# vs and u by seven products each: where late adding transfers, statistics, small constants and weight sums stand in their queues

## The chip, the cores and the metric

The kernel runs on one core of one Trainium2 chip, in one launch. The metric is the device time in microseconds. Times before are the median of 3 runs; the profile is one further execution, with its own time.

## The reference

One layer of a streaming-encoder block on a sequence of 1024 tokens with 1024 features, in float32:

```python
h = rmsnorm(x, norm_g)
q, k, v, za, u, vs, zs, gm = split(h @ w_in)
a = (window_sink_attention(rope(q), rope(k), v, sinks) * silu(za)) @ w_att_out
vs = layernorm(gelu(vs), sg_ln_g, sg_ln_b)                 # along its 1024 features
mixed = einsum('gij,bnjgc->bnigc', masked(sg_w), vs) + sg_b  # 8 groups, blocks of 128 tokens
sgo = (gelu(u) * mixed * silu(zs)) @ w_sg_out
ga, gs = sigmoid(gm + b_merge)
out = rmsnorm(x + (ga * a + gs * sgo) @ w_o, final_g)
```

The mask makes the quarter of each 128 x 128 matrix of `sg_w` zero in which the first 64 tokens would see the last 64.

## The kernel before

Every large product is done by a scheme of Strassen's kind: both factors are cut into 2 x 2 quarters, and seven products of quarters, of sums and of differences of them take the place of eight. The products are called by the form of h that they use: `b11`, `t1`, `t2`, `b21`, `t3`, `b22`, `t4`. Each factor is split into a high part (a cast, ScalarE, line 155) and the rest (a subtraction, VectorE, line 156), and each product takes high x high, high x low and low x high. `product` (line 341) is one such product of 12 matmuls of 128 x 512.

The stages that the change touches, in order:

*vs* (lines 463 to 857). h is formed tile by tile. Its token tiles 4 to 7 give `raw_sum` and `raw_b21`; `add_on` is a transfer on GpSimd's queue that adds to what lies at its target. `raw_t2(t)` (line 603) adds to `raw_sum` on VectorE, and then adds this to `raw_b21` by such a transfer. The quarter `s3` of vs's weights is loaded and gets another quarter added in the same way, in two transfers. `keep_t5` (line 700) copies a product from PSUM into the place of `raw_sum`, so it waits until raw_t2's transfer has read that place. Then come three rounds of `late_product` (matmuls on line 668), with `t2`, `t3` and `t4`: in each, two halves of the weights go over four tiles of tokens. `to_x12` (line 805) and `to_x22` (line 808) add the accumulator to what is kept or subtract it; the next round writes into the same accumulators and waits for them. `aside` is a list of steps on the other engines, one after each group of matmuls: splits of the weights, forms of h for the next round (lines 567 and 568), gelu with the statistics for layernorm (`bn_stats`, line 778). The mixing matrices `mix_w` are loaded early, their masked quarter is set to zero by a memset (line 789), and they are split for the sums of their rows (line 844).

*u* (lines 858 to 939). Eight row tiles of weights in four pairs, `gemm_pair` for each: seven products, in this order, `acc` being one PSUM bank that four of them share:

```python
product(acc, b11); x11 = copy(acc)         # ScalarE, line 359
product(t5, t1);   x22 = -t5               # ScalarE, line 363
product(acc, t2);  x12 = copy(acc)         # ScalarE, line 366; before t3 may write acc
product(t2, b21);  x11 += t2               # VectorE, line 371, term[0]
product(acc, t3);  x22 -= acc              # VectorE, line 376; before t4 may write acc
product(t5, b22);  x12 += t5               # VectorE, line 380
product(acc, t4);  x21 = -acc
```

`finish` applies gelu (line 921) and puts a mix on the list `late`. Between the products, `hook` takes two steps from `late`: first the second statistics of eight tiles and their means (line 866), then `normalize` (a square root on ScalarE, line 135, and eight passes over vs on VectorE, line 871), then mixes: four small matmuls into a bank of two (line 893), gain and bias (line 901), the product with u (line 909) and a store on SP's queue. `split_next` splits the next weights; before it takes the second unit of a pair it makes the four sums of that pair's quarters, s1 to s4 (`sums`, lines 242 to 245), on VectorE. The weights come through three tiles, so a tile of the pair after next is loaded when the splits and sums that read its predecessor are done. `pace` holds a transfer back until a given step.

After u the sinks of the attention are loaded in two transfers (line 932), multiplied by -1 into `nsink` (line 937), and `b_merge` is loaded (line 938); all are used in later stages. Then follow k and v, q, the attention and the rest.

What runs when: a scheduler orders the instructions of each engine from the program's order and its own estimates; `after(second, first)` fixes that the second stands behind the first in their engine's queue, without a wait. Each engine, SP's and GpSimd's transfer queues too, works its queue off in order. TensorE multiplies, VectorE is shown as DVE, ScalarE as ACT, GpSimd as POOL, SyncE as SP.

Of the kernel before, what the change touches and what calls it, by code (L numbers as in the profile page):

```python
# [27 lines left out]
ALU = mybir.AluOpType  # L28
# [24 lines left out]
def hybrid_tile(  # L53
# [16 lines left out]
    nc = tc.nc  # L70
# [8 lines left out]
    def nm(s):  # L79
        count[0] += 1  # L80
        return f"{s}_{count[0]}"

    def bank(tag, dt=F32):
        return psum.tile([P, 512], dt, name=nm("ps_" + tag), tag="ps_" + tag, bufs=2)

    def mtile(shape, dt, tag, bufs, pool=None):
        return (pool or main).tile(shape, dt, name=nm(tag), tag=tag, bufs=bufs)
# [7 lines left out]
    def xtile():  # L95
        return mtile([P, HALF], F32, "x", 5)
# [13 lines left out]
    sink_sb = const.tile([P, 8], F32, name="sink_sb")  # L110
    nsink_sb = const.tile([P, 8], F32, name="nsink_sb")
    bm_sb = const.tile([P, 16], F32, name="bm_sb")
    lg_sb = const.tile([P, KC], F32, name="lg_sb")
    lb_sb = const.tile([P, KC], F32, name="lb_sb")
# [33 lines left out]
    def split(hi, lo, src, minus=False):  # L148
        if minus:
            nc.scalar.mul(hi, src, -1.0)  # L150
            nc.vector.scalar_tensor_tensor(
                lo, src, -1.0, hi.bitcast(F32), op0=ALU.mult, op1=ALU.subtract
            )
        else:
            nc.scalar.copy(hi, src)  # L155
            return nc.vector.tensor_sub(lo, src, hi.bitcast(F32))  # L156

    def after(second, first):

        tc.add_manual_dep(  # L160
            second.ins,
            first.ins.name,
            mybir.DependencyInfo(mybir.DependencyClass.NoSync, mybir.DependencyReason.DATA),
            reason="order",
        )
# [36 lines left out]
    def begin_job():  # L202
        n = len(begun)
        if n < written[0]:
            begun.append(n)
            units.extend(jobs[n]())

    def split_next():

        if not units:  # L210
            begin_job()
        if not units:
            return
        halves, keys = units.pop(0)
        if keys[0][1] == 2:
            make_sums()
        hi = mtile([P, D], F32R, "wh", 3)
        lo = mtile([P, D], F32R, "wl", 3)
        if isinstance(halves, list):
            for c, half in enumerate(halves):  # L220
                split(hi[:, half_of(c)], lo[:, half_of(c)], half)
        else:
            wide = halves.shape[1]
            first = split(hi[:, 0:wide], lo[:, 0:wide], halves)
            if keys[0] == (done[0] - 1, 6) and done[0] > LAST_OF_Q + 2:
                make_sums(first)
        for c, key in enumerate(keys):
            ready[key] = hi[:, half_of(c)], lo[:, half_of(c)]
        if len(units) == 1:
            begin_job()  # L230

    def half_of(half):
        return slice(half * HALF, (half + 1) * HALF)
# [19 lines left out]
    def make_sums(first=None):  # L253

        while sums_to_make:
            sums_to_make.pop(0)(first)
# [23 lines left out]
    def paced(move):  # L280

        if pace[0] is not None:
            tc.add_manual_dep(
                move.ins,
                pace[0].ins.name,
                mybir.DependencyInfo(mybir.DependencyClass.Sync, mybir.DependencyReason.DATA),
                reason="pace",
            )
# [39 lines left out]

    done = [0]
    term = [None]  # L330
    LAST_OF_Q = 8

    def product(acc, part, form, fresh, last=True):
# [16 lines left out]
    def gemm_pair(b, finish, hook=lambda: None, second="o"):  # L350

        n = done[0]
        done[0] += 1
        acc = bank("mm")[:]
        x11, x12, x22 = xtile(), xtile(), xtile()
        product(acc, ready[n, 0], b["b11"], True)
        pace[0] = nc.scalar.copy(x11[:], acc)
        hook()  # L360
        t5 = bank("o")[:]
        product(t5, ready[n, 2], b["t1"], True)
        pace[0] = nc.scalar.mul(x22[:], t5, -1.0)
        hook()
        product(acc, ready[n, 3], b["t2"], False)
        pace[0] = nc.scalar.copy(x12[:], acc)  # L366
        split_next()
        hook()
        t2 = bank(second)[:]
        product(t2, ready[n, 1], b["b21"], True)  # L370
        term[0] = nc.vector.tensor_add(x11[:], x11[:], t2)
        finish(0, 0, x11, x11[:], 1.0)
        split_next()
        hook()
        product(acc, ready[n, 4], b["t3"], False)
        term[0] = nc.vector.tensor_sub(x22[:], x22[:], acc)  # L376
        finish(1, 1, x22, x22[:], 1.0)
        hook()
        product(t5, ready[n, 5], b["b22"], False)
        term[0] = nc.vector.tensor_add(x12[:], x12[:], t5)  # L380
        finish(0, 1, x12, x12[:], 1.0)
        split_next()
        hook()
        product(acc, ready[n, 6], b["t4"], False)
        finish(1, 0, xtile(), acc, -1.0)
        split_next()
        hook()
# [93 lines left out]
    xh = mtile([P, NT, D], F32, "xh", 1, gelu)  # L481
    stats = mtile([P, NT, 2, 6], F32, "bn", 1, gelu)
# [32 lines left out]
    def x_place(i, j, t):  # L515
        return xh[:, 4 * j + t % 4, half_of(i)]
# [4 lines left out]
    def raw_sum(t):  # L521
        return x_place(0, 1, t)

    def raw_b21(t):
        return x_place(1, 0, t)

    g_of = list(g_in)
    casts, lows, turns = [], [], []

    def add_on(dst, src):  # L530
        nc.gpsimd.dma_start(dst, src, accum_op=ALU.add)

    def behind(move, first):
        tc.add_manual_dep(
# [66 lines left out]

    def raw_t2(t):
        nc.vector.tensor_add(raw_sum(t), raw_sum(t), f22[0][:, t - 4, :])
        add_on(raw_b21(t), raw_sum(t))

    def w_vs(i, j, c):
        return w[W_VS + 4 * i + 2 * j + c]

    def two_k(v, c):
        return v[:, 2 * c : 2 * c + 2, :]  # L610

    def flat(v):
        return v.rearrange("p k n -> p (k n)")

    raws = {}
# [13 lines left out]
    def pair_of_w():  # L629
        return mtile([P, D], F32R, "wh", 3), mtile([P, D], F32R, "wl", 3)  # L630

    def keep_w(name, c, hi, lo):
        for k in range(2):
            vs_w[name, 2 * c + k] = hi[:, half_of(k)], lo[:, half_of(k)]

    def split_w(name, c, src=None, behind=False):
        hi, lo = pair_of_w()
        (split_behind if behind else split)(hi[:], lo[:], flat(two_k(raws[name], c)) if src is None else src)
        keep_w(name, c, hi, lo)
# [111 lines left out]
    for t in range(4):  # L751
        to_x11(t)
    for t in (5, 6, 7):
        raw_t2(t)
    load_part("s3", "t4h", 1, 0, True)
    for c in range(2):
        add_on(flat(two_k(raws["s3"], c)), w_vs(0, 0, c))
    by_s4(0)
    by_s4(1)
    a22 = []  # L760
# [14 lines left out]
        keep_t5(t)  # L775

    def statistics(t, half):
        nc.vector.bn_stats(stats[:, t, half, :], xh[:, t, half_of(half)])

    def gelu_of(t, half=0):  # L780
        two = xh[:, t : t + 2, half_of(half)]
        after(nc.scalar.activation(two, two, AF.Gelu), last_cast)
        if half == 0:
            for i in range(2):
                statistics(t + i, 0)

    mix_w = mtile([P, KC, P], F32, "wT", 1, pool)
    behind(nc.sync.dma_start(mix_w[:], sg_w), turns[-1])
    nc.vector.memset(mix_w[64:128, :, 0:64], 0.0)
    ones = mtile([P, P], F32R, "ones", 1, pool)  # L790
    nc.vector.tensor_scalar(ones[:], ident[:], 0.0, 1.0, op0=ALU.mult, op1=ALU.add)

# [35 lines left out]
        + [lambda: gelu_of(0), lambda: gelu_of(2)],  # L828
    )
    row_sums = [bank("sc") for half in range(2)]  # L830
    split_w("s3", 1)
    wh, wl = pair_of_w()
    split(wh[:], wl[:], mix_w[:].rearrange("p g i -> p (g i)"))
    late_product(
# [9 lines left out]
            nc.tensor.matmul(row_sums[half][:], ones[:], part[:, half_of(half)], start=n == 0, stop=n == 1)  # L844
    split_w("a22", 1, a22[1][:])
    part_of_early(1)
    paced(nc.sync.dma_start(lg_sb[:], ln_g))
    paced(nc.sync.dma_start(lb_sb[:], ln_b))
    begin_job()
    late_product("t4", "a22", to_x21, [split_next, lambda: gelu_of(4, 1), lambda: gelu_of(6, 1)])  # L850
    for _ in range(2):
# [7 lines left out]
    def hook():  # L859
        for _ in range(2):  # L860
            if late:
                late.pop(0)()
# [55 lines left out]
    for m in range(0, KC, 2):  # L918

        def finish(i, half, q, src, sign, m=m):  # L920
            nc.scalar.activation(q[:], src, AF.Gelu, scale=sign)
            late.append(lambda: mix(m + i, half, q))
# [3 lines left out]
        gemm_pair(hb, finish, both)  # L926
    while late:
        late.pop(0)()
    of_head = sinks.rearrange("(c e r) -> e c r", e=2, r=2)
    for e in range(2):  # L930
        paced(
            nc.sync.dma_start(
                sink_sb[e * 64 : (e + 1) * 64].rearrange("p (c r) -> p c r", r=2),
                of_head[e].partition_broadcast(64),
            )
        )
    nc.vector.tensor_scalar_mul(nsink_sb[:], sink_sb[:], -1.0)
    paced(nc.sync.dma_start(bm_sb[:], b_merge))
    stage.close()


# [751 lines left out]
    for p in range(4):  # L1693
        acc = bank("sc" if p < 2 else "mm")[:]
        x11 = mtile([P, HALF], F32, gtag(), 1, pool)
# [14 lines left out]
    for p in range(4):  # L1710
        n, t, acc, x11 = N_PAIRS + p, T_ORDER[p], accs[p], firsts[p]
# [173 lines left out]
```

## Time and profile before

| | |
|---|---|
| time, median of 3 runs | 935.46 us (934.58 to 936.62) |
| profiled execution, own time | 937.09 us |
| its span, first to last instruction | 935.3 us |
| mean granted TensorE clock | 0.988 |
| TensorE busy | 903.3 us, 97% of the span |
| VectorE, ScalarE, GpSimd busy | 697.5, 526.4, 141.1 us |
| moved by DMA | 209.57 MB, mean 224 GB/s |

In the views, a row of a timeline gives start and length in us, engine, line, operation, what is written and read, and in brackets how long the engine had stood idle just before, with what ended that. A row of waits gives the engine and line that waited, what ended the wait, the sum in us, how many times, and the longest. A row of windows gives a stretch, its length, the busy time of each engine with its instructions, the granted TensorE clock, the share of time that the DMA engines were busy, and GB/s.

### The profile page before, as it was taken

How to read it: one execution, taken by the hardware profiler on the slowest of the kernel's cores; microseconds unless marked ns; L12 is line 12 of the kernel's file. 1: busy time of each engine (PE TensorE's matmuls, PEld its weight loads, DVE VectorE, ACT ScalarE, POOL GpSimd, SP SyncE). 2: the span in 40 equal slices, each digit the busy share in tenths (PEclk: the TensorE clock that was granted, in tenths of full speed). 3: DMA queues.
4: the chain of work that ended last, by engine and by line, in shares of the span. 5: the costliest groups of instructions: out<-in, count | busy, mean ns of one | idle time of the engine just before them, and what ended most of it. 6: DMA issues, size and time to landing. Idle time of an engine off the chain costs nothing.

```text
span 935.3 us, 13186 instructions
## 1 busy us (share of the span) xinstructions
PE 903.3 (97%) x4284; PEld 749.5 (80%) x4284; DVE 697.5 (75%) x1263; ACT 526.4 (56%) x1058; POOL 141.1 (15%) x204
## 2 busy tenths in 40 slices
PE   8998899979999999999999999999998999999996
PEld 6786778858888778888888888888886887888885
DVE  6868676545668667788878888746798489669996
ACT  6856423323444356776766676746565565458443
POOL 2222112212111001111111111101100011210012
PEclk9999989989999999999999999999999999999999
DMA  9987677974878776778797778899868764999633
GB/s 297 231 216 191 214 225 165 173 149 138 279 236 265 240 210 156 204 201 195 196 221 225 248 216 202 225 290 385 290 237 310 257 200 153 297 290 309 203 109 116
DMA packets 131598, 209.57 MB, mean 224 GB/s; under 512 B 12649, under 2 KB 61033, under 8 KB 131530
## 3 DMA queue, kind: packets, MB, share of 16 engines
q1 hardware_dynamic: 110072, 149.74, 48.5%
q0 software_dynamic: 21312, 58.73, 28.0%
q8 instruction: 34, 0.56, 0.2%
q14 instruction: 34, 0.28, 0.1%
q10 hardware_dynamic: 146, 0.27, 0.1%
HBM read 147.74 MB, written 86.11 MB: 250 GB/s over the span
## 4 chain that ended last, share of the span: by engine, by line
PE 76%; DVE 10%; DMA 8%; issue 3%; ACT 2%; SPq 1%; DVEq 0%; POOL 0%; ACTq 0%; POOLq 0%
PE ps_mm L341 34%; PE ps_o L341 24%; DMA wr<-in_w_dram 4%; PE ps_sc L1215 3%; PE ps_tp L341 3%; PE ps_o L1300 2%; PE ps_sc L341 2%; PE ps_tp L1259 2%; DVE wl L156 2%; PE ps_o L668 2%; DMA xh<-xh 1%; DMA sink_sb<-in_sinks_dram 1%; DVE bq L185 1%; PE ps_sc L556 1%; PE ps_mm L668 1%
## 5 line engine op out<-in xcount | busy, mean ns | idle before, releaser
L155 ACT CAST wh<-s 128x1024 fp32r<-128x1024 f32 (+1 forms) x78 | 78.2, 1004 | 85.7 <-PE ps_mm L341 46.8
L156 DVE TENSOR_TENSOR wl<-wr,wh 128x1024 fp32r<-128x1024 f32 (+1 forms) x78 | 73.1, 940 | 48.5 <-ACT wh L155 47.8
L156 DVE TENSOR_TENSOR wl<-s,wh 128x1024 fp32r<-128x1024 f32 (+1 forms) x78 | 91.6, 1175 | 9.2 <-ACT wh L155 9.0
L155 ACT CAST wh<-wr 128x1024 fp32r<-128x1024 f32 (+1 forms) x78 | 64.0, 823 | 60.0 <-PE ps_mm L341 33.1
L341 PE MATMUL ps_mm<-T_t4h,wh 128*128 128x512 f32 x140 | 56.5, 403 | 7.8 <-DVE x L376 7.7
L341 PE MATMUL ps_o<-T_t1h,wh 128*128 128x512 f32 x148 | 58.8, 398 | 0.7 <-ACT wh L155 0.7
L341 PE MATMUL ps_o<-T_b22h,wh 128*128 128x512 f32 x148 | 58.5, 395 | 0.0
L341 PE MATMUL ps_mm<-T_t3h,wh 128*128 128x512 f32 x140 | 55.5, 396 | 2.9 <-ACT x L366 2.9
L341 PE MATMUL ps_mm<-T_b11h,wl 128*128 128x512 f32 x140 | 55.2, 395 | 2.9 <-DVE wl L156 2.9
L341 PE MATMUL ps_o<-T_b22l,wh 128*128 128x512 f32 x148 | 57.9, 391 | 0.0
L341 PE MATMUL ps_o<-T_b22h,wl 128*128 128x512 f32 x148 | 57.8, 390 | 0.0
L341 PE MATMUL ps_o<-T_t1h,wl 128*128 128x512 f32 x148 | 57.7, 390 | 0.0
L341 PE MATMUL ps_o<-T_t1l,wh 128*128 128x512 f32 x148 | 57.6, 390 | 0.0
L341 PE MATMUL ps_mm<-T_t4h,wl 128*128 128x512 f32 x140 | 55.7, 398 | 0.0
L341 PE MATMUL ps_mm<-T_t4l,wh 128*128 128x512 f32 x140 | 55.7, 398 | 0.0
L341 PE MATMUL ps_mm<-T_t3l,wh 128*128 128x512 f32 x140 | 55.1, 393 | 0.6 <-DVE T_t3l L156 0.6
L341 PE MATMUL ps_mm<-T_b11h,wh 128*128 128x512 f32 x140 | 55.6, 397 | 0.0
L341 PE MATMUL ps_mm<-T_t3h,wl 128*128 128x512 f32 x140 | 55.3, 395 | 0.0
L341 PE MATMUL ps_mm<-T_t2h,wl 128*128 128x512 f32 x140 | 55.3, 395 | 0.0
L341 PE MATMUL ps_mm<-T_t2l,wh 128*128 128x512 f32 x140 | 55.2, 395 | 0.0
L341 PE MATMUL ps_mm<-T_b11l,wh 128*128 128x512 f32 x140 | 55.1, 394 | 0.0
L341 PE MATMUL ps_mm<-T_t2h,wh 128*128 128x512 f32 x140 | 55.0, 393 | 0.0
(384 smaller groups left out, 2399.4 us busy)
## 6 DMA issues: line engine op xcount, KB each, us to landing
wr<-in_w_dram SPq DMA_DIRECT2D x86, 256.0 KB
sums<-in_w_dram POOLq DMA_DIRECT2D x20, 512.0 KB, 8.0
s<-sums SPq DMA_DIRECT2D x20, 512.0 KB
q_hl<-qhl SPq DMA_DIRECT2D x16, 512.0 KB
q<-q_hl SPq DMA_DIRECT2D x64, 128.0 KB
y_dr<-x POOLq DMA_DIRECT2D x28, 256.0 KB, 6.4
wr<-in_w_dram SPq DMA_DIRECT2D x12, 512.0 KB
g<-in_w_dram POOLq DMA_DIRECT2D x12, 512.0 KB, 6.4
```

What stands on the lines that cost most here:

```text
L155: nc.scalar.copy(hi, src)
L156: return nc.vector.tensor_sub(lo, src, hi.bitcast(F32))
L185: op(dst[:, i : i + 2, :], a[:, i : i + 2, :], c[:, i : i + 2, :])
L341: nc.tensor.matmul(acc, lt, rt, start=fresh and k == 0 and n == 0, stop=k == 3 and n == 2, skip_group_check=True,)
L556: turns.append(nc.tensor.transpose(pt[:, i * P : (i + 1) * P], xt[:, k * P : (k + 1) * P], ident[:]))
L668: mm = nc.tensor.matmul(acc[:], lt, rt, start=fresh and k == 0 and n == 0, stop=k == 3 and n == 2, skip_group_check=True,)
L1215: nc.tensor.matmul(sc[:, i, k0:], q_of[:, c, i * P : (i + 1) * P], kt[:, f, k0:], start=f == 0, stop=f == 1,)
L1259: nc.tensor.transpose(dst, pr[:, i, block * P : block * P + width], ident[:])
L1300: nc.tensor.matmul(po[:, cs], lt, rt, start=n == 0, stop=n == len(terms) - 1)
```

## The change

Nothing is computed otherwise, and no instruction is added or removed. Seven things move:

1. The last `raw_t2` transfer stands ahead of the two that add to `s3` on GpSimd's queue.
2. The early statistics (half 0) stand behind the low halves of `t3` or `t4` that were last formed when they are written down.
3. The memset in `mix_w` stands behind the same, after the split of `s3`'s second half.
4. The gains and offsets of layernorm, `b_merge` and the sinks are loaded between the rounds `t2` and `t3` of vs, held back until round `t2`'s last matmul; before, the first two came after round `t3`, the others after u.
5. `nsink` stands behind the last term of u's pairs on VectorE.
6. The sums of the weights for u's second, third and fourth pair, and for the pair of k and v, have s1 and s3 behind the term of x11 (line 371) of the pair before; before, they had no such place.
7. With these, the scheduler's order on SP's queue moves too: the loads of a pair's second tile of weights stand behind two stores of mixes. On TensorE the first two matmuls of u's second pair come ahead of two mixes.

```diff
@@ split_next
         if keys[0][1] == 2:
-            make_sums()
+            make_sums(term_of_x11[0] if done[0] <= 4 else None)
@@
     term = [None]
+    term_of_x11 = [None]
@@ gemm_pair
-        term[0] = nc.vector.tensor_add(x11[:], x11[:], t2)
+        term[0] = term_of_x11[0] = nc.vector.tensor_add(x11[:], x11[:], t2)
@@
     def add_on(dst, src):
-        nc.gpsimd.dma_start(dst, src, accum_op=ALU.add)
+        return nc.gpsimd.dma_start(dst, src, accum_op=ALU.add)
@@ raw_t2
-        add_on(raw_b21(t), raw_sum(t))
+        return add_on(raw_b21(t), raw_sum(t))
@@
     for t in (5, 6, 7):
-        raw_t2(t)
+        last_of_h = raw_t2(t)
     load_part("s3", "t4h", 1, 0, True)
     for c in range(2):
-        add_on(flat(two_k(raws["s3"], c)), w_vs(0, 0, c))
+        after(add_on(flat(two_k(raws["s3"], c)), w_vs(0, 0, c)), last_of_h)
@@
     def statistics(t, half):
-        nc.vector.bn_stats(stats[:, t, half, :], xh[:, t, half_of(half)])
+        return nc.vector.bn_stats(stats[:, t, half, :], xh[:, t, half_of(half)])
@@ gelu_of
-                statistics(t + i, 0)
+                after(statistics(t + i, 0), lows[-1])
@@
     behind(nc.sync.dma_start(mix_w[:], sg_w), turns[-1])
-    nc.vector.memset(mix_w[64:128, :, 0:64], 0.0)
@@ after round t2
     row_sums = [bank("sc") for half in range(2)]
+    paced(nc.sync.dma_start(lg_sb[:], ln_g))
+    paced(nc.sync.dma_start(lb_sb[:], ln_b))
+    paced(nc.sync.dma_start(bm_sb[:], b_merge))
+    of_head = sinks.rearrange("(c e r) -> e c r", e=2, r=2)
+    for e in range(2):
+        paced(
+            nc.sync.dma_start(
+                sink_sb[e * 64 : (e + 1) * 64].rearrange("p (c r) -> p c r", r=2),
+                of_head[e].partition_broadcast(64),
+            )
+        )
     split_w("s3", 1)
+    after(nc.vector.memset(mix_w[64:128, :, 0:64], 0.0), lows[-1])
@@ after round t3
     part_of_early(1)
-    paced(nc.sync.dma_start(lg_sb[:], ln_g))
-    paced(nc.sync.dma_start(lb_sb[:], ln_b))
@@ after u
-    of_head = sinks.rearrange("(c e r) -> e c r", e=2, r=2)
-    for e in range(2):
-        paced(
-            nc.sync.dma_start(
-                sink_sb[e * 64 : (e + 1) * 64].rearrange("p (c r) -> p c r", r=2),
-                of_head[e].partition_broadcast(64),
-            )
-        )
-    nc.vector.tensor_scalar_mul(nsink_sb[:], sink_sb[:], -1.0)
-    paced(nc.sync.dma_start(bm_sb[:], b_merge))
+    after(nc.vector.tensor_scalar_mul(nsink_sb[:], sink_sb[:], -1.0), term[0])
```

## The prediction

> **What bounds the kernel now.** I read the page first, then TensorE's own waits, then the stretches around them as windows, and last the timeline just ahead of each wait.
>
> ```profile
> span 935.3 us, 13186 instructions
> PE 903.3 (97%) x4284; PEld 749.5 (80%) x4284; DVE 697.5 (75%) x1263; ACT 526.4 (56%) x1058; POOL 141.1 (15%) x204
> PE ps_mm L341 <- DVE x L376: 6.7, 1, 6.7
> PE ps_mm L341 <- ACT x L366: 2.9, 1, 2.9
> PE ps_tp L893 <- DVE x L909: 1.8, 1, 1.8
> PE ps_mm L668 <- DVE xh L805: 1.7, 1, 1.7
> PE ps_tp L668 <- ACT T_t4h L567: 0.6, 1, 0.6
> PE ps_mm L668 <- DVE wl L156: 0.5, 1, 0.5
> ```
>
> The first two lines are the page's, the other six TensorE's waits between 40 and 310 us. TensorE is busy 97% of the span, so the kernel is bound by its matmuls plus the holes between them. The six holes lie where the diff works: in vs's products (L668) and in u's pairs of rows (L341, L893). They sum to 14.2 us, but a hole also costs what the clock loses behind it, and only windows show that. Their columns are the length, each engine's busy time, the granted clock, the DMA engines' share and GB/s.
>
> ```profile
> 64.40:77.96 13.56, 11.36 (x49) 8.78 (x48) 7.27 (x11) 7.68 (x11) 2.86 (x4) 1.00 0.98 237
> 77.96:90.70 12.74, 12.18 (x53) 9.76 (x53) 12.74 (x19) 6.58 (x9) 2.54 (x4) 1.00 0.56 154
> 90.70:101.58 10.88, 10.88 (x50) 9.01 (x48) 10.35 (x21) 6.16 (x8) 2.67 (x5) 1.00 0.92 254
> 101.58:115.47 13.89, 11.04 (x49) 8.82 (x47) 6.81 (x19) 5.14 (x9) 1.55 (x3) 1.00 0.56 195
> 115.47:127.80 12.33, 12.21 (x52) 9.73 (x52) 11.22 (x17) 5.06 (x7) 3.29 (x5) 0.86 0.96 265
> 127.80:135.86 8.06, 6.23 (x28) 5.59 (x29) 6.43 (x10) 1.39 (x2) 0.00 (x0) 0.79 0.47 180
> 156.10:178.71 22.61, 22.61 (x117) 19.10 (x116) 15.21 (x23) 7.40 (x12) 5.80 (x7) 1.00 0.86 148
> 178.71:198.10 19.39, 19.39 (x99) 16.25 (x97) 9.36 (x13) 4.64 (x8) 5.80 (x7) 1.00 0.88 174
> 198.10:204.88 6.78, 0.04 (x1) 0.00 (x0) 0.84 (x3) 0.02 (x1) 0.00 (x0) 0.80 0.86 201
> 204.88:210.43 5.55, 5.54 (x20) 4.54 (x21) 5.45 (x8) 2.96 (x4) 0.00 (x0) 0.63 0.20 69
> ```
>
> The yardstick is 156.10 to 178.71, the third pair of u: seven products and four mixes in 22.61 us, no hole, full clock. Against it stand three places.
>
> - A, vs's second and third product round, 64.40 to 90.70: busy 11.36 of 13.56 and 12.18 of 12.74, so 2.20 + 0.56 = 2.76 us are holes, at full clock.
> - B, the first pair and the first product of the second, 101.58 to 135.86: 13.89 + 12.33 + 8.06 = 34.28 us.
> - C, the fourth pair, 178.71 to 210.43: 19.39 + 6.78 + 5.55 = 31.72 us, which is 9.11 over the yardstick. 6.7 of it is one hole; the rest is the clock at 0.63 behind it.
>
> **The change part by part.** Part A: the adding transfer of raw_t2 goes ahead of the two that make s3, and the memset of mix_w and the early statistics go behind the splits.
>
> ```profile
> 59.23 0.86 POOL L531 DMA_DIRECT2D T_t4h<-in_w_dram  x1 [0.80 <-DMA T_t4h<-in_w_dram]
> 59.77 1.22 POOL L531 DMA_DIRECT2D xh<-xh  x1
> 68.02 0.48 DVE L789 MEMSET wT<- 64x512 f32 x1 [5.21 <-DMA wT<-in_sg_w_dram]
> 72.03 0.59 ACT L700 COPY xh<-ps_sc 128x512 f32<-128x512 f32 x1 [5.44 <-DMA xh<-xh]
> 77.13 0.68 DVE L805 TENSOR_TENSOR xh<-xh,ps_mm 128x512 f32<-128x512 f32 x1
> 77.96 0.70 PE L668 MATMUL ps_mm<-wh,T_t3h 128*128 128x512 f32 x2 [1.68 <-DVE xh L805]
> 111.13 0.69 DVE L778 BATCH_NORM_STATS2 bn<-xh 128x6 f32<-128x512 f32 x1
> 161.60 2.72 PE ps_mm L341 x12
> ```
>
> (All from the timeline but the last, which is from the chain: one product of 12 matmuls.) GpSimd's queue is in order: the last xh<-xh transfer stood behind both adds on T_t4h, which waited for their loads, and the copy L700 on ScalarE waited 5.44 us for it, to 72.03. Behind L700 are queued the casts of s3 and of t3; behind those on VectorE, L805; and TensorE waited for L805 (1.68). In the changed program xh<-xh is issued some 2 us earlier and lands earlier still, so L700 runs when ScalarE reaches it, at 66.6 (72.03 less 5.44). VectorE no longer stands 5.21 us before the memset, so the low half of s2 is ready when its cast is and the 0.5 hole goes. Two things could be late next. The adds on T_t4h go out at most 1.22 us later; all three transfers had landed by 72.03, so in the new order they have too. L805 started 5.1 us behind L700 in the trace (77.13 against 72.03); with the first add down by 69.5, as I estimate, it starts by 74.6, against a need at 75.3 (64.40 and 48 matmuls at 2.72 us for 12). The other is VectorE, busy for all 12.74 us of 77.96 to 90.70: it gets the memset (0.48) and three statistics (0.69 each) more there, 2.5 us, and begins that round's work about 2.5 us sooner, so it comes out even. Bounds: 0 to 2.76 gained; I take 1.8.
>
> Part B: the sums of the second pair's weights move behind L371 (term_of_x11), away from the statistics.
>
> ```profile
> 99.05 11.38 DMA wr<-in_w_dram
> 110.52 0.69 DVE L242 TENSOR_TENSOR s<-wr 128x512 f32<-128x512 f32 x1 [6.98 <-DMA wr<-in_w_dram]
> 113.73 0.21 ACT L135 ACTIVATE st<-st 128x8 f32<-128x8 f32 x1 [7.35 <-DVE st L133]
> 114.83 0.59 ACT L366 COPY x<-ps_mm 128x512 f32<-128x512 f32 x1
> 115.85 3.03 DVE L871 TENSOR_SCALAR xh<-xh,mv,st 128x1024 f32<-128x1024 f32 x4
> 123.31 0.80 DVE L871 TENSOR_SCALAR xh<-xh,mv,st 128x1024 f32<-128x1024 f32 x1
> 126.35 1.23 DVE L156 TENSOR_TENSOR wl<-s,wh 128x1024 fp32r<-128x1024 f32 x1 [1.04 <-ACT wh L155]
> 129.63 3.01 PE L893 MATMUL ps_tp<-wT,xh 128*128 128x128 f32 x16 [1.85 <-DVE x L909]
> ```
>
> (The first line is from the chain, the others from the timeline.) A sum that needed a weight still in flight held VectorE 6.98 us, with the last statistic (at 111.13) behind it; the square root L135 therefore held ScalarE 7.35 us, the copy L366 was late, and t3's product waited 2.9. The normalising pass (L871) ran late too, so the mixes came late and waited 1.85 for L909. B without trouble is a yardstick pair and one more product: 22.61 + 2.72 = 25.33, so B holds 34.28 - 25.33 = 8.95 us. Of these 4.75 are the two holes and 4.20 the clock, at 0.86 and 0.79.
>
> Trainium skill, "TensorE: Matmul & The Clock Gate", section "Part 1: The HAM clock gate": the array drops to half clock after an idle window of about 3.4 us. Here holes of 2.9 and 1.85 us were followed by 0.86 and 0.79, so the trace disagrees with that length as a threshold. By that rule of the Trainium skill B's two holes would be worth 4.75 and the whole sum would be 4.20 less.
>
> What is late next in B: without its wait VectorE is free at 110.52 - 6.98 = 103.5, and a statistic, a split (1.23) and a little more make the root's input ready near 105.5; normalising then starts at about 106.7 instead of 115.85. From there to the last of it took 123.31 + 0.80 - 115.85 = 8.3 us, hence 115; the mixes are due after six products, at 101.58 + 6 x 2.72 = 117.9. Then VectorE has L376, three sums, L380, the fourth sum, a split of 1.23 and two mixes' tails before L909 (some 7.5 us at 0.6 to 0.7 each): 122.5 to 123, and TensorE needs the mixing bank at 123. So the margin is nothing, and a hole like the 1.85 may stay: bounds 0 and 1.85 plus its share of the clock, 3.5; I take 1.2 and count 7.8 for B.
>
> Part C: the sinks' loads go up to before the third round, and nsink behind the last term of u's pairs.
>
> ```profile
> 193.49 0.62 SPq L932 DMA_DIRECT2D sink_sb<-in_sinks_dram  x1
> 203.35 0.54 SPq L200 DMA_DIRECT2D wr<-in_w_dram  x1
> 204.04 0.17 DVE L937 TENSOR_SCALAR nsink_sb<-sink_sb 128x8 f32<-128x8 f32 x1 [10.57 <-DMA sink_sb<-in_sinks_dram]
> 204.14 0.69 DVE L376 TENSOR_TENSOR x<-x,ps_mm 128x512 f32<-128x512 f32 x1
> 204.88 0.79 PE L341 MATMUL ps_mm<-T_t4h,wh 128*128 128x512 f32 x1 [6.75 <-DVE x L376]
> 208.60 0.68 DVE L242 TENSOR_TENSOR s<-wr 128x512 f32<-128x512 f32 x1
> ```
>
> An 8-column multiply waited 10.57 us for 4 KB, with L376 behind it and t4's product behind that: 9.11 us. In the changed program these loads, with the norm's gains and b_merge, leave SP at about 76, the sinks over 100 us before L937. SP issues five instead of two there (0.62 for one), some 3 us in front of loads that wait longer anyway for a buffer; the cover is that wait, and without it the 3 us would fall on the first pair's second tile, needed only at 93. What can be late next are the sums of the first q pair: L242 at 208.60 used loads issued up to 203.35. Now the fourth sum frees their buffer some 5 us later in the pair (by the program's order, just ahead of L380), while the DMA share stands at 0.88, and VectorE waits with t3's split behind it, needed 11 us into the k and v pair. I see 0 to 4 us for that, and take 0.8: 8.3 for C.
>
> Sum: 1.8 + 7.8 + 8.3 = 17.9, say 18. Nothing is added or removed in number; the moved memset, statistics and sums run in time that VectorE now spends waiting. Against the profiled execution's own 937.1 us (its span is 935.3) this gives 919.1; that execution is 1.6 us above the median of the runs, 935.46, so for the median 917.5.
>
> **The rivals.**
>
> *Late weights.* Every sum for pairs two to five now stands in VectorE's queue between L371 and L376, and the fourth sum frees a tile for the next load about 5.5 us later than the split did. If a load lands late, L376 is late and TensorE waits again. For it: the DMA share was 0.86 to 0.98 through most of this stretch, and by the windows the same transfers must fit into some 18 us less. Against it: from the fourth sum (about 18.5 us into a pair, where the sixth product ends) to the next use (behind the fourth product of the following one, 11.5) are 22.61 - 18.5 + 11.5 = 15.6 us, and another 4 pass before t4's product needs L376; the load that ended VectorE's 6.98 wait was on its way for 11.38. It would give back about half: 926.5.
>
> *The slow clock has another cause.* Then the low clock in B stays, and only holes go: 4.20 less, 921.7. This is also what the Trainium skill's rule, in the section named above, would give. Against it: both slow stretches begin right behind holes, and the yardstick has neither.
>
> *Slower.* The same mechanism in its strong form: the loads of all four pairs take over 20 us, L376 waits in each, and each hole drags the clock down. To lose the 20.8 us that A, B and C hold, each pair must wait over 3 us and lose 2 more to the clock, so loads of about 24 us, twice what the trace shows. It would give 940.
>
> *It doesn't do what it says.* The DMA engines, not the order, set A to C, and the holes move without shrinking: 935. Against it: the DMA share was 0.56 while TensorE stood in B and 0.20 behind C.
>
> **How the numbers follow.** Forecast, 14 to 22 us gained: 0.68. Late weights: 0.17. The clock: 0.04. No effect: 0.03. Slower: 0.08. The forecast's own range is 913.5 to 921.5; reaching up to 927 takes in most of the late weights and leaves under 2 in 10 out. A measurement of this kernel tells about 0.2% (1.9 us) from no change. Faster by more than that: 0.89; within: 0.03; slower: 0.08.
>
> **What would show it.** Right: L700 without its 5.44; L135 waiting under 2 us; no wait for DMA at nsink; the pair around C at 22.6 us; PE's waits of the list down to some 2 us; the first pair and a product at 25 to 28 us. Wrong: waits of L242 for in_w_dram ahead of L376 with TensorE waiting for L376 or for the mixing bank in several pairs, a clock under 0.9 in pairs two to four, or a wait on T_t4h's adds in A.

## The result, and the profile after

The changed kernel took 923.88 us (median of 4 runs, 919.77 to 924.99) against 935.66 us on the same chip: ratio 0.9866, interval [0.9833, 0.99]. That is 11.8 us gained where the forecast had 18; the profiled execution went from 937.09 to 924.99, its span from 935.3 to 923.2.

The page of the changed kernel, its two lines that answer to those of before:

```profile
span 923.2 us, 13181 instructions
PE 898.0 (97%) x4284; PEld 746.0 (81%) x4284; DVE 697.0 (75%) x1263; ACT 527.3 (57%) x1058; POOL 141.4 (15%) x204
```

The counts of the five rows are those of before; the whole count is five lower, and the page does not say which five.

TensorE's waits of the changed kernel, 40 to 310 us:

```profile
PE ps_mm L342 <- ACT xh L811: 3.8, 1, 3.8
PE ps_o L669 <- ACT xh L687: 3.0, 1, 3.0
PE ps_tp L903 <- DVE x L919: 0.4, 1, 0.4
```

All six holes of before are gone (0.4 is left of the mixes' 1.8). Two others stand there: 3.8 us where u's first product waits for the gelu L811, and 3.0 us at L687, in a part of vs that the change does not touch. Line numbers up to about 700 are one higher than before, those of the late part of vs and of u up to ten (L366 is L367, L376 is L377, L871 is L881, L893 is L903, L909 is L919).

Windows of the changed kernel, columns as in the prediction: A's two rounds, the stretch behind the hole at L811, the first pair and a product (B), and the pairs from 154.66 and from 177.51 us (the latter holds C's place):

```profile
69.06:82.62 13.56, 13.56 (x61) 11.26 (x60) 9.06 (x14) 8.74 (x12) 2.87 (x4) 1.00 1.02 257
82.62:95.30 12.68, 12.68 (x57) 10.47 (x56) 12.30 (x18) 9.06 (x11) 3.81 (x6) 1.00 0.67 165
106.57:110.00 3.43, 3.43 (x10) 2.75 (x11) 3.43 (x9) 2.34 (x4) 0.00 (x0) 0.66 0.84 309
106.57:134.58 28.01, 27.62 (x129) 22.92 (x130) 27.59 (x53) 12.85 (x18) 4.13 (x7) 0.94 0.70 232
154.66:177.51 22.85, 22.85 (x117) 19.35 (x117) 15.02 (x23) 7.64 (x13) 5.80 (x7) 1.00 0.82 151
177.51:200.36 22.85, 22.85 (x118) 19.34 (x117) 13.96 (x20) 7.64 (x13) 5.80 (x7) 1.00 0.94 190
```

A is full and so are the pairs. B took 28.01 where a pair and a product are 22.85 + 2.72 = 25.57; the excess of 2.44 is mostly the clock at 0.66 behind the new hole. The timeline of the changed kernel shows how that hole comes about:

```profile
80.98 0.43 SPq L833 DMA_DIRECT2D bm_sb<-in_b_merge_dram  x1
81.45 1.40 SPq L837 DMA_DIRECT2D sink_sb<-in_sinks_dram  x2
90.06 1.09 SPq L200 DMA_DIRECT2D wr<-in_w_dram  x2
102.97 0.69 DVE L242 TENSOR_TENSOR s<-wr 128x512 f32<-128x512 f32 x1 [5.90 <-DMA wr<-in_w_dram]
104.97 1.04 ACT L155 CAST wh<-s 128x1024 fp32r<-128x1024 f32 x1 [9.80 <-DVE s L243]
106.57 0.50 PE L342 MATMUL ps_mm<-T_b11h,wh 128*128 128x512 f32 x1 [3.78 <-ACT xh L811]
113.70 0.21 ACT L135 ACTIVATE st<-st 128x8 f32<-128x8 f32 x1 [0.65 <-DVE st L133]
```

The second tile of weights of u's first pair left SP at 90.06. VectorE waited 5.90 us for it, to 102.97; ScalarE stood 9.80 us in front of the cast of its sum, with L811 queued behind that; L811 gives TensorE its bank back. Before, the same tile left SP at 89.61 and its sum ran at 95.44 without a wait. So the load that took under 6 us now took over 12. L135, the step that B was to free, waited 0.65.

### The profile page after: what moved, and what is told of

The parts are those of the page before. It is cut to its first block, busy times and chain, and to the rows that moved or that the text cites. A ratio compares the mean times of both kernels' runs of the same rounds, so it can differ in the third digit from the quotient of the medians.

```text
span 923.2 us, 13181 instructions
## 1 busy us (share of the span) xinstructions
PE 898.0 (97%) x4284; PEld 746.0 (81%) x4284; DVE 697.0 (75%) x1263; ACT 527.3 (57%) x1058; POOL 141.4 (15%) x204
## 4 chain that ended last, share of the span: by engine, by line
PE 75%; DVE 10%; DMA 9%; issue 2%; ACT 1%; SPq 1%; POOL 0%; DVEq 0%; ACTq 0%; POOLq 0%
PE ps_mm L342 35%; PE ps_o L342 25%; PE ps_sc L1216 3%; DMA T_t4h<-in_w_dram 3%; PE ps_tp L342 3%; PE ps_o L1301 2%; PE ps_sc L342 2%; DMA wr<-in_w_dram 2%; PE ps_tp L1260 2%; DVE wl L156 2%; PE ps_tp L903 1%; DMA T_t3h<-T_t4h 1%; DVE bq L185 1%; DMA T_t3l<-T_t3h 1%; DVE bn L779 1%
## 5 line engine op out<-in xcount | busy, mean ns | idle before, releaser
L1229 ACT ACTIVATE pr<-ps_sc,sm 128x192 f32<-128x192 f32 (+2 forms) x128 | 50.9, 410 | 6.6 <-DVE sm L1225 5.5
```

The source lines that it names most:

```text
L1229: nc.scalar.activation(held_in[c, i], sc[:, i, lo:hi], AF.Exp, bias=nmax[:, c, i : i + 1], scale=-1.0, accum_out=sums[:, c, i : i + 1],)
```

## The experiments

All ran beside the kernel before; its medians were 934.82 us for the first four kernels, 934.95 for the next four, 935.26 for the three after and 934.25 for the last.

### Small loads behind round t3 (e1_small_after_t3)

```diff
@@ between rounds t2 and t3
-    (five small loads: gains, offsets, b_merge, two of the sinks)
@@ after round t3
     part_of_early(1)
+    (the same five)
     begin_job()
```

> The changed kernel, with its five small loads (norm's gains and offsets, b_merge, two of the sinks) written down after round t3 in place of after round t2: on SP's queue they come behind the loads of the first pair's second tile of weights, and nothing else moves on any engine. In the changed kernel that tile's second half took 12.43 us from its issue, L242 on VectorE waited 5.90 us for it, and TensorE 3.8 us for the gelu L811 before u's first product. Queue theory (the small loads ahead of it on the same queue held it up): the load lands in under 7 us, L242's wait for it is under 1 us, TensorE does not wait for L811, and the time falls by 4 to 6 us, the clock behind the hole included: 918 to 920. Contention theory (the adding transfers keep the DMA engines full between 92 and 103, whatever stands ahead): the load still takes 10 to 13 us, the hole stays at 3 to 4 us, and the time stays within 1.5 us of 923.9. Against the kernel before: ratio 0.981 to 0.983 by the first, 0.986 to 0.988 by the second.

Measured: 915.0 us (913.3 to 917.28), 0.9793 [0.9771, 0.9816], disjoint from the changed kernel's interval and faster than either theory had it. In TensorE's waits the list of 40 to 310 us is down to this:

```profile
PE ps_mm L342 <- DVE x L377: 0.6, 1, 0.6
PE ps_o L669 <- ACT xh L687: 0.2, 1, 0.2
```

So the place of five loads, 20 KB in all, decides over 7 to 9 us (915.0 against 923.88, and against 921.8 when the changed kernel ran again, below). I first read this as SP's queue: what stands ahead of the tile holds it. The later runs took that back.

### The parts alone (e2_constants_only, e3_sums_only, e4_vs_only)

Each adds one part of the change to the kernel before. Items 4 and 5 (small loads, `nsink`), then item 6 (sums), then items 1 to 3 (vs):

```diff
+    (five small loads between rounds t2 and t3)
+    after(nc.vector.tensor_scalar_mul(nsink_sb[:], sink_sb[:], -1.0), term[0])
```

> The kernel before, with the change of the small constants alone: the five small loads after round t2, nsink behind the last term of u's pairs. Part C of the prediction: L937 waits for nothing, the hole of 6.7 us ahead of t4's product of the fourth pair goes with the slow clock behind it, 8 to 9 us gained. Queue theory: the second tile's load lands late here too (10 to 13 us after its issue in place of under 6), so part of this is given back in front of u's first product; B's hole of 2.9 us changes its place at most. Net 925 to 929. Contention theory: nothing is given back, 926 to 927.5, and L242's first wait in u stays under 1 us.

```diff
-            make_sums()
+            make_sums(term_of_x11[0] if done[0] <= 4 else None)
```

> The kernel before, with the sums' new place alone (s1 and s3 behind the term of x11 of the pair before). Part B of the prediction, by itself: L135 no longer waits some 7 us, the hole of 2.9 us before the first pair's t3 goes, of the 1.85 us before the mixes 0 to 1.2 stays, the sinks' hole of 6.7 us stays. Gain 6 to 9 us: 927 to 930. Rival (the sums behind x11 only move the wait into the pair): gain under 3 us, with L376 waiting for a sum that waits for its weights.

```diff
+        after(add_on(flat(two_k(raws["s3"], c)), w_vs(0, 0, c)), last_of_h)
+                after(statistics(t + i, 0), lows[-1])
+    after(nc.vector.memset(mix_w[64:128, :, 0:64], 0.0), lows[-1])
```

> The kernel before, with the changes in vs alone: raw_t2's last transfer ahead of the adds on s3, the early statistics and the memset of mix_w behind the splits. Part A of the prediction: L700 waits under 1 us in place of 5.44, the holes of 0.5, 1.7 and 0.6 us in rounds t2 and t3 go, gain 1.8 to 2.8 us: 933 to 934. The copy L700 must now be followed by a wait of the first cast of s3 for its adding transfer, some 2 us long, without a hole in TensorE. Rival (B takes it back: what comes 2.8 us sooner waits at the same load of weights, which landed at 110.4): gain under 0.5 us, with a hole before the first pair's t3 of more than 4 us.

Measured: 926.47 (0.9926 [0.9903, 0.995]), 920.09 (0.9847 [0.9824, 0.987]) and 927.46 (0.9923 [0.9905, 0.9941]). They gained 8.4, 14.7 and 7.4 us, 30.5 in all; together, with the small loads in their better place, they gain 19.8. The last two took clearly less time than I expected (920.09 for 927 to 930, 927.46 for 933 to 934), and their traces say why: the scheduler sets VectorE's order anew with each edit. With the sums alone, VectorE's timeline has:

```profile
187.80 0.68 DVE L377 TENSOR_TENSOR x<-x,ps_mm 128x512 f32<-128x512 f32 x1
196.70 0.17 DVE L938 TENSOR_SCALAR nsink_sb<-sink_sb 128x8 f32<-128x8 f32 x1 [2.96 <-DMA sink_sb<-in_sinks_dram]
```

`nsink`, which before stood ahead of the term L376, now stands behind it, so that its wait stops nobody: C's hole went without C. With vs's part alone, VectorE has the last step of the statistics ahead of the second pair's sums (before: 113.54 against 110.52):

```profile
101.70 0.16 DVE L133 TENSOR_SCALAR st<-mv 128x8 f32<-128x8 f32 x1
104.64 0.69 DVE L242 TENSOR_TENSOR s<-wr 128x512 f32<-128x512 f32 x1 [2.27 <-DMA wr<-in_w_dram]
```

so most of B's stall went without B (1.6 us of holes in the pair instead of 4.75).

In e2 the small loads leave SP ahead of the same tile, and its sum ran at 95.79 without a wait. There the holes of A still stood: the adding transfers of round t3 were issued more slowly (77.11, 81.61 and 85.13 us, against one every 2.72), and they landed in 5.8 to 6.3 us. If the small loads make a pause there, it fell into a gap; this is an inference.

### The changed kernel again, and three ways to move the small loads

```diff
# e5_after_again: nothing
# e6_sinks_behind: the two loads of the sinks go behind round t3, the other three stay
# e7_scalar_queue: all five stay, but
-    paced(nc.sync.dma_start(...))
+    paced(nc.scalar.dma_start(...))
```

> The changed kernel itself, unchanged, beside the others and the kernel before on one chip. Theory 1, the five small loads hold the first pair's second tile: 920 to 925, the sum L242 waits 3 us or more for in_w_dram around 100 us, and the first product of u waits for the gelu L811. Theory 2, that wait belonged to one execution in which vs's adding transfers had slipped by 4.7 us: no wait of L687 and none of L811, and 914 to 917, as with the small loads behind round t3 (915.0).

> The changed kernel with only the two loads of the sinks put behind the loads of the first pair's second tile; the gains of the norm and b_merge stay ahead of it. If the sinks hold the queue (512 of the some 900 small packets are theirs, 8 bytes each): within 2 us of 915.0 and no wait of L811. If any small load ahead of the tile does it: 919 to 924, L242 still waiting 2 us or more for its load. If only the traffic of the adding transfers does it: like the changed kernel, 920 to 925.

> The changed kernel with the five small loads at the same place of the program, but issued by ScalarE to its own queue. If the tile waits for small packets ahead of it in SP's queue: L242 no longer waits for its load beyond 1 us, and 915 to 918 (the five issues take ScalarE some 2 us, which may show in front of t4's pieces). If the small packets disturb the tile wherever they are queued, by what they take from the DMA engines: 920 to 925 and the wait of L242 stays at 3 us or more.

Measured: e5 921.8 us (0.9859 [0.9838, 0.9879]), e6 914.25 (0.9776 [0.9758, 0.9793]), e7 923.18 (0.9874 [0.9852, 0.9897]). So the wait is the kernel's, not one execution's: in e5 L242 waits 5.0 us and TensorE 2.8. Its list of TensorE's waits, and behind it that of e6:

```profile
PE ps_mm L342 <- ACT xh L811: 2.8, 1, 2.8
PE ps_o L669 <- ACT xh L687: 1.6, 1, 1.6
PE ps_tp L903 <- DVE x L919: 0.4, 1, 0.4
```

```profile
PE ps_mm L342 <- DVE x L377: 1.0, 1, 1.0
PE ps_o L669 <- ACT xh L687: 0.2, 1, 0.2
```

It is the sinks; with them behind the tile, both are gone. And it is not SP's queue: from ScalarE's queue the same loads do the same, with none of them ahead of the tile on SP. TensorE's wait and VectorE's timeline of e7:

```profile
PE ps_mm L342 <- ACT xh L811: 5.8, 1, 5.8
```

```profile
101.02 0.69 DVE L242 TENSOR_TENSOR s<-wr 128x512 f32<-128x512 f32 x1 [7.99 <-DMA wr<-in_w_dram]
```

The Trainium skill, "DMA: Bandwidth & Descriptors", section "Issuing engines are not separate DMA queues", says that transfers run on the same 16 DMA engines and interleave whoever starts them. e7 agrees: 923.18 against 923.88 and 921.8.

What the small pieces do is seen in the DMA engines. A window of 2 us some 3 us behind the last small load in e5, and one at about the same place of the program in e6 (the last two columns are the DMA share and GB/s):

```profile
82.00:84.00 2.00, 2.00 (x10) 1.67 (x9) 1.82 (x3) 2.00 (x4) 0.69 (x1) 1.00 0.18 15
```

```profile
81.00:83.00 2.00, 2.00 (x10) 1.66 (x9) 1.82 (x4) 2.00 (x4) 0.69 (x1) 1.00 0.72 195
```

The engines are hardly busy and move few bytes, although GpSimd issues an adding transfer of 512 KB every 2.72 us. A low share alone is no sign of harm: the kernel before has 0.12 from 80 to 82 us, with no small load near and landings of 5.3 us. It is the landing that tells. The issues of DMA in five such microseconds give the median time to landing of two of them, first e5, then e6:

```profile
sums<-in_w_dram POOLq DMA_DIRECT2D x2, 512.0 KB, 9.9
```

```profile
sums<-in_w_dram POOLq DMA_DIRECT2D x2, 512.0 KB, 6.4
```

By the time the tile leaves SP, the late adding transfers share the engines with it. That this backlog is what slows the tile is the reading that fits all runs; it was not cut apart by itself. Behind the tile the sinks seem to slow the adding transfers too, but nothing is due soon there: issued from 88 to 94 us, these land in 14.1 (e1) and 11.4 us (e6), against 9.0 in e10 (below) and 8.8 in e4, which load no sinks there.

### How many small pieces (e10_wide_sinks, e11_half_sinks, e12_gains_behind)

```diff
# e10: one load of 64-byte rows, sorted ahead of nsink on VectorE
-    (two loads of the sinks, pieces of 8 bytes)
+    paced(nc.sync.dma_start(sink_all[:], sinks.partition_broadcast(P)))
+    after(nc.vector.tensor_copy(...), term[0])      # twice
# e11: one of the two loads of the sinks goes behind round t3
# e12: both stay, the other three loads go behind round t3
```

> The changed kernel, small loads at its own place, with the sinks loaded as one transfer of 64-byte rows to 128 partitions (128 packets) in place of two with 512 pieces of 8 bytes, and sorted into their two halves by two small copies on VectorE ahead of nsink (0.2 us each). If the number of small packets does it: 913 to 916, adding transfers issued between 75 and 86 us land in 5.5 to 7 us, and L242 does not wait. If the bytes, or any transfer at that place, do it: 920 to 925 like the changed kernel, with landings of 9 us or more.

> The changed kernel with one of the two loads of the sinks at its own place and the other behind the loads of the first pair's second tile: half of the 8-byte pieces ahead. If each piece costs its share: 916 to 920, adding transfers issued meanwhile landing in 7 to 8.5 us, and a wait of L242 between 0 and 4 us. If it takes all of them to matter (the tile has some slack): 914 to 915. If any of them do it: 920 to 924.

> The mirror of the version with the sinks behind: the sinks' two loads (512 pieces of 8 bytes) stay at the changed kernel's place, and the norm's gains and b_merge (some 384 pieces of 32 and 64 bytes) go behind the loads of the first pair's second tile. If it is the number of small pieces in a row (some 900 hold the DMA engines up, 640 and fewer did not): 912 to 916, adding transfers issued just behind the sinks landing in 6 to 7.5 us, no wait of L242. If it is the sinks' two loads together, whatever stands ahead of them: 920 to 924, landings of 9 us or more and a wait of L242 of 3 us or more.

Beside the others (packets: counted on the queue that issues the small loads, from their issue to the tile's; landing: as above, in the 5 us behind the small loads; wait: of L242 for the first pair's second tile):

| kernel | packets | loads of 8-byte pieces | landing, us | wait, us | time, us |
|---|---|---|---|---|---|
| changed kernel | 976 | 2 | 10.8 | 5.90 | 923.88 |
| e5, the same | 976 | 2 | 9.9 | 5.02 | 921.8 |
| e7, ScalarE's queue | 976 | 2 | 11.2 | 7.99 | 923.18 |
| e12 | 541 | 2 | 9.7 | 2.15 | 917.68 |
| e11 | 704 | 1 | 6.6 | none | 913.74 |
| e10 | 576 | 0 | 6.9 | none | 915.77 |
| e6 | 432 | 0 | 6.4 | none | 914.25 |

The intervals are 0.9792 [0.9768, 0.9815] for e10, 0.9768 [0.9744, 0.9792] for e11, and 0.9825 [0.98, 0.985] for e12. Not the number of packets: 541 with both loads of 8-byte pieces slow the adding transfers, 704 with one do not. It takes both loads of the sinks, and with the other pieces ahead of them it is worse. e12 came out between its two theories: the adding transfers are as late as the second says, the tile less so. There TensorE no longer waits for L811; the late tile seems to put the statistics back instead (L135 waits 2.20), and the mixes wait:

```profile
PE ps_tp L903 <- DVE x L919: 2.0, 1, 2.0
```

The Trainium skill, "DMA: Bandwidth & Descriptors", section "Rules for kernel authors", says that a last dimension that is not contiguous becomes one descriptor per element and should be made contiguous. The sinks' pieces are two neighbouring elements each, so the rule fits them only in kind; e10, which reads whole rows at the price of two copies of 0.17 us, is in keeping with it: 915.77. Many partitions that read the same address are not enough to do harm, since in e10 all 128 read the same 64 bytes. Whether it is the 8 bytes of each piece, or that 512 pieces read the same 64 bytes, no run tells.

### Each part with the others in place (e8_no_vs, e9_no_sums)

```diff
# on e1: e8 takes items 1 to 3 back (not shown), e9 takes item 6 back:
-            make_sums(term_of_x11[0] if done[0] <= 4 else None)
+            make_sums()
```

> The version with the small loads behind round t3 (915.0), with part A undone: adding transfers, memset and statistics of vs as in the kernel before; sums and small loads as in that version. If the parts add up as the prediction's sum has them, A is worth 1.8: 916 to 918. If the moved sums alone already do B's and C's work (they brought 14.7 by themselves) and A is then worth its hole and the rounds behind it: 919 to 921, with a hole of 2.5 to 3 us at L806 and no hole at L367, L377 or L919.

> The version with all five small loads behind round t3 (915.0), with the move of u's sums (part B) undone. If the parts add up as the prediction's sum has them, B is worth 7.8: 922 to 924, with the holes of 2.9 at L367 and 1.8 at L919. If the moved work of vs already takes most of B's stall away, as its trace by itself suggests (there VectorE has the statistics ahead of the sums, and only 1.6 us of holes are left in u's first pair): 915 to 918, and no wait over 1.5 us in TensorE's list between 40 and 310 us.

Measured: e8 920.02 (0.9832 [0.9812, 0.9851]), e9 921.7 (0.9862 [0.9832, 0.9891]), against 915.0 with all. A is worth 5.0 us there by the medians, 3.6 by the ratios, whose intervals just touch; both are above 1.8, which the intervals alone hardly exclude, and the trace is as the second theory has it. Its hole is longer than before (2.6 against 1.68), and the window behind it shows half the clock: 2.6 and some 1.4 us by the trace. TensorE's waits and the window of e8:

```profile
PE ps_mm L669 <- DVE xh L806: 2.6, 1, 2.6
```

```profile
79.13:82.00 2.87, 2.87 (x7) 2.29 (x8) 2.87 (x5) 1.11 (x2) 0.00 (x0) 0.50 0.47 84
```

B is worth 6.7 by the medians. My second theory for e9 (915 to 918) fell, and the holes are not where the first put them. TensorE's waits of e9, and its VectorE:

```profile
PE ps_tp L903 <- DVE xh L881: 4.7, 7, 2.0
```

```profile
110.25 0.69 DVE L242 TENSOR_TENSOR s<-wr 128x512 f32<-128x512 f32 x1 [7.65 <-DMA wr<-in_w_dram]
```

With the statistics done at 101.93, it is the normalising pass that now stands behind the sums, and the mixes wait for it. In e4, with the same order on VectorE but the sinks still behind u, the wait was 2.27; so the sinks, now behind the first pair's tile, seem to hold up the second pair's (adding transfers issued from 88 to 94 us land in 13.5 us in e9, in 8.8 in e4). In e1 the same sum stands behind L372 by item 6, runs at 112.60 and waits for nothing: the place behind round t3 is free only with item 6.

## Why the prediction came out as it did

The median, 923.88, is 6.4 us above the forecast of 917.5. It lies outside the forecast's own range (913.5 to 921.5) and inside the wider one that reaches up to 927 for the rival of late weights. It was faster by more than 0.2%, as the likeliest case said. That it fell inside the wider range is in part luck: the room was left for loads of the later pairs, and another load took it.

Of the signs of being right, these came: L700 without its wait, L135 at 0.65, no wait for DMA at `nsink`, the pair around C near 22.6 (22.85). Two did not: TensorE's list sums to 7.2 us and not some 2, and the first pair and a product took 28.01. One of the signs of being wrong came as well, a wait on T_t4h's adds in A.

**A: right, the size above the value taken.** ScalarE's timeline of the changed kernel:

```profile
71.14 0.58 ACT L701 COPY xh<-ps_sc 128x512 f32<-128x512 f32 x1
73.70 1.05 ACT L155 CAST wh<-T_t4h 128x1024 fp32r<-128x1024 f32 x1 [1.98 <-DMA T_t4h<-in_w_dram]
```

L700 (now L701) runs without its 5.44. The first cast of s3 waits 1.98 for its add, but TensorE does not feel it, and both rounds are full. In e6, where the rounds begin within 0.3 us of those of before, the copy runs at 66.57 (66.6 in the prediction) and the first add lets that cast start at 69.03 (69.5). So 2.76 of holes are gone where 1.8 was taken.

**B and C: right, with the stated sizes a little low.** Where the sinks are out of the way (e6), windows of the first pair with a product, and of the pair that held C:

```profile
98.21:123.89 25.68, 25.65 (x130) 21.53 (x129) 25.39 (x49) 12.05 (x16) 5.12 (x8) 1.00 0.94 310
166.82:189.67 22.85, 22.85 (x117) 19.34 (x117) 13.95 (x20) 7.63 (x13) 5.80 (x7) 1.00 0.93 193
```

B went from 34.28 to 25.68, 8.6 us against 7.8, and C from 31.72 to 22.85, 8.9 against 8.3. With A's 2.76 this is 20.2, and e6 gained 20.7. So the sum of 17.9 was sound for what it counted, place by place. Which edit does it is less clear for C: the sums alone removed its hole too (e3), and no run takes C back with the others in place. The wait that C put at 0 to 4 us, for the sum of the first q pair, came as well (4.13 us of VectorE at 203.56 in the changed kernel, 5.20 in e6); TensorE did not feel it.

**The step that failed is in part C: what the small loads cost where they go to.** It priced their issue on SP, 3 us under the cover of a wait for a buffer, and the issue did cost nothing: the tile's loads left SP at 90.06 in the changed kernel and at 85.40 in e6, and the whole stretch lies 4.4 us earlier in e6 (rounds from 69.06 and from 64.64). It did not price the pieces behind the issues. With them the adding transfers landed late, and the tile that was "needed only at 93" came at 103. With the sinks out of the way the time is 7.5 to 9.6 us lower (914.25 against 921.8 and 923.88), but not all of that is theirs.

Compared place by place, the changed kernel is 10.7 us behind e6 where the third pair begins (154.66 against 143.97): 4.6 are there before u's first product would have begun (106.57 - 3.78 against 98.21), 3.78 are the hole at L811, and 2.3 follow in the pair behind it, mostly clock. In e5 the same three are 1.7, 2.8 and 2.3, in e7 0.6, 5.8 and 2.5. So the sinks cost 6.1, 5.1 and 8.3 us by these traces. The 4.6 and 1.7 come from the hole at L687 (3.0 and 1.6 us), which both profiles of the changed kernel have and the twelve others, the kernel before among them, have at 0.2. In the changed kernel ScalarE stood just ahead of it, with L687 queued behind:

```profile
42.80 1.04 ACT L572 CAST wh<-T_t3l 128x1024 fp32r<-128x1024 f32 x1 [2.71 <-DMA T_t3l<-T_t3h]
```

In e5 this first cast waits 1.33 us for the same adding transfer, in the twelve others not at all. The order of work on VectorE and ScalarE up to there is the same in all, and the small loads leave SP over 30 us later; why the transfer was late in those two stays open.

**The rivals.** Late weights was the right kind of mechanism, one load that lands late and TensorE behind it, at another place: the first pair's second tile, not the later pairs'. The sums for pairs two to four and for k and v waited for nothing in the changed kernel, with the DMA share at 0.82 and 0.94. That the slow clock had a cause of its own fell: with the holes gone the clock is 1.00 in both windows of e6, and it fell to 0.66 behind the new hole. No effect and slower fell as well.

**What I did not see.** The prediction took the parts as additive. The places add up, as shown above for e6, but the edits do not. They are in part substitutes: alone 8.4, 14.7 and 7.4, with the others in place 5.0 for A and 6.7 for B. In e3 and e4 the scheduler moves `nsink` or the statistics out of the way when another edit alone is made.

**The version that beats both kernels** is the changed kernel with the sinks moved or loaded as whole rows, in any of four ways (e1, e6, e10, e11): 913.7 to 915.8 us, intervals overlapping.

## What to carry to other kernels

When small loads are moved out of a stall, price their pieces and not only their issue: ask which large transfers run just then, and who needs those next. Loads broken into many 8-byte pieces (512 did harm here, 256 did not) belong behind the last load that is due soon, or should be made of whole rows and sorted on chip, as e10 does. When a scheduler sets the order, test the parts of a change alone and with the others in place before adding them up.

## What the runs showed of the hardware that I had not expected

- 4 KB of sinks in 8-byte pieces, in two loads, with other small loads ahead, brought the DMA engines down to 15 GB/s at a share of 0.18 for 2 us (e5), and adding transfers of 512 KB from 6.4 to about 10 us; from another queue it was the same (11.2). One of the two loads alone did nothing of the kind (6.6), nor did all five where the adding transfers came more slowly (e2, 5.8 to 6.3).
- The clock behind a hole: holes of 1.60 us (e5, L687), 1.68 (before, L805) and 1.83 (e2, L918) left it at 1.00; one of 1.89 (e2, L366) was followed by 0.60 for 2.14 us, one of 2.03 (e12) by 0.66 (the 1.85 before by 0.79), one of 2.61 (e8) by 0.50 for 2.87 us, one of 2.97 (L687 in the changed kernel) by 0.56 for 3.10.
